# Hybrid decoder layer on one core: three plain column blocks in place of two ahead of the seven-product loop, and a later split of the first down chunk

## The chip, the cores and the metric

One core of one Trainium2 chip. The metric is the device time of one execution in microseconds (us), as the median of several runs; a profile of one execution stands beside it.

## The reference

One layer on 512 tokens of width 1024, float32: a mixer with attention and retention heads, then cross-attention to 256 memory rows, then a gated feed-forward part, each with a norm ahead, a norm behind and a residual. The change lies in the feed-forward part and in the last rows of the cross-attention ahead of it:

```python
FFN_HIDDEN = 2816

def swiglu(h, w_gate_up, w_down):
    g, u = jnp.split(h @ w_gate_up, 2, axis=-1)
    return (jax.nn.silu(g) * u) @ w_down

y = memory_cross_attn(rms_norm(x, pre_mem_g[l]), mem, mem_norm_g[l],
                      w_q_mem[l], w_kv_mem[l], w_o_mem[l])
x = x + rms_norm(y, post_mem_g[l])
y = swiglu(rms_norm(x, pre_ffn_g[l]), w_gate_up[l], w_down[l])
x = x + rms_norm(y, post_ffn_g[l])
```

## The kernel before

Each float32 operand is split into a high part and the rest (`split`, lines 88 to 94: ScalarE casts, VectorE subtracts), and each product is three matmuls (`mm3`, lines 82 to 86): high by high, high by rest, rest by high.

The tokens are four row blocks of 128. `mem_block` (line 855) does the out projection of the cross-attention for one row block, its residual and the next norm, and gives `h`. `to_b` (line 861) transposes `h` on TensorE and splits it into `B11` and `B21` (row blocks 0 and 1, the two halves of the width) or `B12` and `B22` (row blocks 2 and 3). For row blocks 2 and 3 it also forms `t1` to `t4`, differences of these. Their splits into `T1` to `T4` come later (`late_splits`). Row block 2 does its subtractions on GpSimd, row block 3 on VectorE.

The hidden width of 2816 is 22 column blocks of 128, numbered `f`. Each has 128 gate columns and 128 up columns, which lie in HBM as four parts a11, a12, a22, a21 of 512. Gate and up for all tokens are a product of two 2 by 2 block matrices, and there are two ways to get it:

- `plain` (line 993): eight block products, 24 matmuls of 256 columns for each of gate and up and for each half of the tokens, 96 in all. Its first half (`n` 0) needs row blocks 0 and 1 alone, the second (`n` 1) needs `B12` and `B22`. It takes a pair `was[f]` over all 2048 columns, made by `blocks_a(f, 2048, 512)`.
- `step` (line 948): seven block products with sums of blocks, 84 matmuls of 256 columns. It takes `was[f]` over 1536 columns and `wbs[f]`, the split of `sums[f]`.

`blocks_fetch` (line 110) loads a raw block from SP's queue into one of two buffers. `blocks_a` (line 127) casts it on ScalarE (L131), negates the cast (L134), and lets an accumulating DMA from GpSimd's queue add the raw block from HBM to it (L135), so that the rest is left. `blocks_sum` (line 115) forms s1 and s2 on VectorE, s3 and s4 on GpSimd. `blocks_b` splits one half of the sums.

Blocks 0 and 1 are plain (`PRE = 2`, line 991). The order written at lines 1000 to 1031 is: fetch and `blocks_a` of both, fetch of block 2, first halves of both with `to_b` of row block 2 between them, `to_b` of row block 3, `blocks_a` and sums of block 2, second halves of both, each followed by the silu product (L1023, L1024) and its store, then block 3. Here a scheduler orders the instructions when it compiles, by program order and by when it takes them to be ready. Blocks 2 to 21 run in `step` under a fixed order, the order of the text.

Within a step, products 1 and 2 go to the two halves of bank `p`. ScalarE copies the first half to `s1` (`ffn_c1`, line 927), and VectorE adds the second half (`ffn_c11`, line 931, the addition `c L933`). Products 4 and 6 go to `q` and `r`, then `s L979` reads `r`; 5 goes to `q`; 7 overwrites the first half of `p`; 3 goes to the second half of `r`. Between the copy and the addition the step splits half of the next block's sums. In block 21 there is no next block, and `load()` (line 142), which splits the first chunk of w_down, stands there instead:

```python
    if nxt:
        blocks_b(f + 1, 1)
    else:
        load()
    ffn_c11(f)
    q, r = bank("q2"), bank("r")
```

SBUF holds twenty units of 8 KB a partition (`unit`, line 57): a pair is two of them, a chunk of w_o is a pair, x is two units of two row blocks. x is stored to HBM (L1034) before the loop, which frees its units. PSUM has eight banks (`bank`, line 54).

After the loop the down projection (`down`, line 1061) runs 528 matmuls of 512 columns, and the last residual ends the kernel.

Of the kernel before, what the change touches and what calls it, by code (L numbers as in the profile page):

```python
# [38 lines left out]
def hybrid_layer(ctx, tc, t, out):  # L39
# [10 lines left out]
    def uname(p):  # L50
        cnt[0] += 1
        return f"{p}{cnt[0]}"

    def bank(name):
        return psp.tile([P, 512], F32, tag="ps", name=uname(name))

    def unit(name, dt=F32):
        return up.tile([P, 2048], dt, tag="u", name=uname(name))

    def pair(name):  # L60
        return unit(name + "h", F32R), unit(name + "l", F32R)

    def work(name):
        return wk.tile([P, 512], F32, tag="w2k", name=uname(name))
# [14 lines left out]
    def part(pr, c0, n):  # L79
        return pr[0][:, c0:c0 + n], pr[1][:, c0:c0 + n]  # L80
# [7 lines left out]
    def split(src, hi, lo, scale=None):  # L88
        if scale is None:
            nc.scalar.copy(hi, src)  # L90
            nc.vector.tensor_sub(lo, src, hi.bitcast(F32))  # L91
        else:
            nc.scalar.mul(hi, src, scale)
            nc.vector.scalar_tensor_tensor(lo, src, scale, hi.bitcast(F32), op0=ALU.mult, op1=ALU.subtract)
# [6 lines left out]
    def fetch(key):  # L101
        fetched[key] = raw = rawp.tile([P, 2048], F32, tag="raw", name=uname("raw"))
        nc.sync.dma_start(raw, t[key[0]][key[1]])
# [6 lines left out]
    def blocks_fetch(f):  # L110
        chunks.remove(("w_gu", f))
        raws[f] = rawp.tile([P, 2048], F32, tag="raw", name=uname("raw"))
        nc.sync.dma_start(raws[f], t["w_gu"][f])

    def blocks_sum(f, names):
        if f not in sums:
            sums[f] = unit("sums")
        a11, a12, a22, a21 = (raws[f][:, i * 512:(i + 1) * 512] for i in range(4))
        s2, s4, s1, s3 = (sums[f][:, i * 512:(i + 1) * 512] for i in range(4))
        for name in names:  # L120
            e = nc.gpsimd if name in ('s3', 's4') else nc.vector
            if name == "s1":
                e.tensor_add(s1, a21, a22)
            else:
                e.tensor_sub(*{"s2": (s2, s1, a11), "s3": (s3, a11, a21), "s4": (s4, a12, s2)}[name])  # L125

    def blocks_a(f, n=1536, m=768):
        w = was[f] = pair("wa")
        for c0 in range(0, n, m):
            c = slice(c0, c0 + m)  # L130
            nc.scalar.copy(w[0][:, c], raws[f][:, c])  # L131
        for c0 in range(0, n, m):
            c = slice(c0, c0 + m)
            nc.scalar.mul(w[1][:, c], w[0][:, c].bitcast(F32), -1.0)  # L134
        nc.gpsimd.dma_start(w[1][:, :n], t["w_gu"][f][:, :n], accum_op=ALU.add)  # L135

    def blocks_b(f, i):
        if f not in wbs:
            wbs[f] = pair("wb")
        split(sums[f][:, i * 1024:(i + 1) * 1024], *part(wbs[f], i * 1024, 1024))  # L140

    def load(pieces=1, swap=False):
        key = chunks.pop(0)
        src = t[key[0]][key[1]]
        raw = fetched.pop(key, None)
        w = pair("w")
        if raw is None:
            raw = rawp.tile([P, 2048], F32, tag="raw", name=uname("raw"))
            n = 2048 // pieces
            for i in range(pieces):  # L150
                c = slice(i * n, (i + 1) * n)
                nc.sync.dma_start(raw[:, c], src[:, c])
        n = 2048 // max(2, pieces)
        for i in range(max(2, pieces)):
            c = slice(i * n, (i + 1) * n)
            if swap and i == 0:
                nc.vector.tensor_copy(w[0][:, c], raw[:, c])
                nc.vector.tensor_sub(w[1][:, c], raw[:, c], w[0][:, c].bitcast(F32))
            else:
                split(raw[:, c], w[0][:, c], w[1][:, c])  # L160
        loaded[key] = w
# [750 lines left out]
    def product(i, w, ps):  # L912
        u, c0, name = prods[i]
        for k in range(4):
            x_ = bx[name][:, k * H:(k + 1) * H], bx[name][:, 1024 + k * H:1024 + (k + 1) * H]
            mm3(ps, part(w[u], c0 + k * P, P), x_, k == 0, k == 3)
# [3 lines left out]
    def ffn_p12(f):  # L920

        w, p = (was[f], wbs[f]), bank("p")
        product(1, w, p[:, :H])
        product(2, w, p[:, H:])
        ffn[f] = w, p, work("s1"), work("c"), work("u")

    def ffn_c1(f):
        w, p, s1, c, u = ffn[f]
        nc.scalar.copy(s1[:, :H], p[:, :H])

    def ffn_c11(f):
        w, p, s1, c, u = ffn[f]
        nc.vector.tensor_add(c[:, :H], s1[:, :H], p[:, H:])  # L933

    def ffn_done(f):
        w, p, s1, c, u, r = ffn[f]
        nc.vector.tensor_add(c[:, H:], c[:, H:], r[:, H:])  # L937
        nc.scalar.activation(c, c, AF.Silu)  # L938

    def keep(f, v):  # L940
        nc.sync.dma_start(ad[:, f * S:(f + 1) * S], v)

    def ffn_mult(f):
        c, u = ffn.pop(f)[3:5]
        nc.vector.tensor_mul(c, c, u)
        keep(f, c)

    def step(f):
        nxt = f + 1 < FT
        two = f + 2 < FT  # L950
        ffn_p12(f)
        w, p, s1, c, u = ffn[f]
        if f + 3 < FT:
            blocks_fetch(f + 3)
        else:
            fetch(("w_dn", f + 3 - FT))
        if f > PRE:
            ffn_done(f - 1)
        if two:
            blocks_sum(f + 2, ("s3", "s1", "s2"))  # L960
        ffn_c1(f)
        if f > PRE:
            ffn_mult(f - 1)
        if nxt:
            blocks_b(f + 1, 1)
        else:
            load()
        ffn_c11(f)
        q, r = bank("q2"), bank("r")
        ffn[f] += (r,)  # L970
        product(4, w, q[:, :H])
        product(6, w, r[:, :H])
        if two:
            blocks_sum(f + 2, ("s4",))
        if nxt:
            blocks_b(f + 1, 0)
        if two:
            blocks_a(f + 2)
        nc.vector.tensor_add(s1[:, H:], s1[:, :H], r[:, :H])  # L979
        product(5, w, q[:, H:])  # L980
        nc.vector.tensor_add(c[:, H:], s1[:, H:], q[:, H:])
        product(7, w, p[:, :H])
        nc.vector.tensor_add(s1[:, :H], s1[:, H:], p[:, :H])
        nc.vector.tensor_add(u.rearrange("p (i s) -> p i s", i=2), q.rearrange("p (i s) -> p i s", i=2),
                             s1[:, None, :H].to_broadcast([P, 2, H]))
        product(3, w, r[:, H:])
        for d in (raws, was, sums, wbs):
            d.pop(f, None)


    PRE = 2

    def plain(f, j, n, ps):
        for i, (c0, name) in enumerate(((0, "B1%d"), (512, "B2%d")) if j == 0 else ((1536, "B1%d"), (1024, "B2%d"))):
            v = bx[name % (n + 1)]
            for k in range(4):
                mm3(ps[:, n * H:(n + 1) * H], part(was[f], c0 + k * P, P),
                    (v[:, k * H:(k + 1) * H], v[:, 1024 + k * H:1024 + (k + 1) * H]), i == k == 0, i == 1 and k == 3)

    pg = {f: (bank("g"), bank("u")) for f in range(PRE)}  # L1000
    for f in range(PRE):
        blocks_fetch(f)
        blocks_a(f, 2048, 512)
    blocks_fetch(2)
    for f in range(PRE):
        for j in range(2):
            plain(f, j, 0, pg[f][j])
        if f == 0:
            late_splits = [to_b(hb, 2, nc.gpsimd)]
    late_splits.append(to_b(hc, 3))  # L1010
    blocks_a(2)
    blocks_sum(2, ("s3", "s1", "s2", "s4"))
    blocks_fetch(3)
    for f in range(PRE):
        for j in range(2):
            plain(f, j, 1, pg[f][j])
        if f == 0:
            for e in late_splits:
                e()
            late_splits.clear()  # L1020
        del was[f], raws[f]
        sg = work("sg")
        nc.scalar.activation(sg, pg[f][0], AF.Silu)  # L1023
        nc.vector.tensor_mul(sg, sg, pg[f][1])  # L1024
        keep(f, sg)
        blocks_b(2, 1 - f)
    pg.clear()
    del bx["B12"]
    blocks_a(3)
    blocks_sum(3, ("s3", "s1", "s2", "s4"))  # L1030
    blocks_fetch(4)
    xd = tc.dram_tile([S, D], F32, name="xd")
    for b in range(TB):
        nc.sync.dma_start(xd[b * P:(b + 1) * P, :], x[b])  # L1034
# [13 lines left out]
    with tc.manual_schedule():  # L1048
        for f in range(PRE, FT):
            step(f)  # L1050
            if f == FT - 2:
                split_a(0)
        ffn_done(FT - 1)
        ffn_mult(FT - 1)
# [130 lines left out]
```

## Time and profile before

| what | us |
|---|---|
| median of 3 runs | 802.81 |
| all runs | 955.97, 802.81, 799.59 |
| profiled execution, own time | 801.05 |
| its span, first to last instruction | 799.3 |
| TensorE busy in the span | 780.2 |
| VectorE busy | 502.5 |
| ScalarE busy | 386.4 |
| GpSimd busy | 201.1 |
| DMA, mean of the span | 151 GB/s |

Matmuls overlap one another, and each is shown longer than its distance to the next; the distance is read from starts. The feed-forward part begins at 439.69 with the first plain block; the loop runs from 465.25 to 672.23, the down projection from 672.23 to 792.11.

### The profile page before, as it was taken

Reading aid. Unit: us, or ns where it says so; the run is one execution under the profiler, and the core shown is the slowest. Engines: PE = TensorE matmul, PEld = TensorE weight load, DVE = VectorE, ACT = ScalarE, POOL = GpSimd, SP = SyncE. Lnnn points to the kernel's source line nnn. Section 1 sums busy time; section 2 is a strip of 40 time slices with the busy share of each in tenths; the row PEclk is TensorE's granted clock in tenths of the full one; section 3 lists DMA queues with packets and bytes.
Section 4 is the critical chain, followed back from the end, with each engine's and each line's share of the span. In section 5 each row is a group of like instructions: output and inputs, shape, how many; then the busy total and the mean of one; then the engine's idle time right before and its main releaser. Section 6 shows DMA issues by size and latency. Waiting matters only on the chain.

```text
span 799.3 us, 12220 instructions
## 1 busy us (share of the span) xinstructions
PE 780.2 (98%) x4828; PEld 695.8 (87%) x4828; DVE 502.5 (63%) x1002; ACT 386.4 (48%) x667; POOL 201.1 (25%) x177
## 2 busy tenths in 40 slices
PE   9999999899999999999999989999999999999996
PEld 7788888777887888999988989999999998888885
DVE  6497368574666657757567797667777767541143
ACT  6522424485563824445437575555555545542011
POOL 0163033420111100400000654333333326551000
PEclk9999999989999999999999999999999999999999
DMA  8634313223135430525008288777777793864011
GB/s 324 268 132 155 109 53 106 66 79 119 54 106 204 170 154 0 182 83 192 19 28 214 80 243 220 208 210 206 208 208 205 208 267 117 310 250 171 1 52 53
DMA packets 24489, 120.60 MB, mean 151 GB/s; under 512 B 2928, under 2 KB 2928, under 8 KB 14960
## 3 DMA queue, kind: packets, MB, share of 16 engines
q1 hardware_dynamic: 19904, 99.89, 34.3%
q0 software_dynamic: 3808, 18.88, 12.6%
q10 hardware_dynamic: 720, 1.06, 0.4%
q8 instruction: 38, 0.62, 0.3%
q14 instruction: 19, 0.16, 0.1%
HBM read 108.80 MB, written 9.96 MB: 149 GB/s over the span
## 4 chain that ended last, share of the span: by engine, by line
PE 52%; DVE 4%; issue 0%; ACT 0%; DVEq 0%; ACTq 0%
PE dn L84 5%; PE dn L85 5%; PE dn L86 5%; PE p L84 3%; PE p L86 3%; PE p L85 3%; PE q L85 3%; PE q L86 3%; PE q L84 3%; PE r L84 2%; PE r L86 2%; PE r L85 2%; PE o L84 2%; PE o L85 2%; PE o L86 2%; DVE wbl L91 1%
## 5 line engine op out<-in xcount | busy, mean ns | idle before, releaser
L91 DVE TENSOR_TENSOR wl<-raw,wh 128x1024 fp32r<-128x1024 f32 (+1 forms) x91 | 120.0, 1354 | 69.1 <-ACT wh L90 39.0
L90 ACT CAST wh<-raw 128x1024 fp32r<-128x1024 f32 (+1 forms) x91 | 90.0, 1038 | 61.4 <-DMA raw<-in_w_in 29.3
L91 DVE TENSOR_TENSOR wbl<-sums,wbh 128x1024 fp32r<-128x1024 f32 x40 | 51.2, 1280 | 30.3 <-ACT wbh L90 30.3
L84 PE MATMUL dn<-wh,ah 128*128 128x512 f32 x176 | 68.5, 389 | 0.0
L85 PE MATMUL dn<-wl,ah 128*128 128x512 f32 x176 | 68.5, 389 | 0.0
L86 PE MATMUL dn<-wh,al 128*128 128x512 f32 x176 | 68.5, 389 | 0.0
L135 POOL DMA_DIRECT2D wal<-in_w_gu x22 | 19.5, 887 | 176.1 <-ACT wal L134 117.5
L1045 POOL TENSOR_TENSOR al<-af,ah 128x512 fp32r<-128x512 f32 x22 | 36.1, 1673 | 43.9 <-ACT ah L1044 43.9
L84 PE MATMUL p<-bB,wah 128*128 128x256 f32 x160 | 45.3, 283 | 0.0
L85 PE MATMUL p<-bB,wah 128*128 128x256 f32 x160 | 45.3, 283 | 0.0
L86 PE MATMUL p<-bB,wal 128*128 128x256 f32 x160 | 45.3, 283 | 0.0
L90 ACT CAST wbh<-sums 128x1024 fp32r<-128x1024 f32 x40 | 40.2, 1051 | 3.4 <-POOL sums L125 1.8
L125 POOL TENSOR_TENSOR sums<-raw,sums 128x512 f32<-128x512 f32 x20 | 34.1, 1705 | 25.4 <-DVE sums L125 25.4
L86 PEld LDWEIGHTS dn<-wh,al 128*128 128x128 f32 x176 | 33.0, 188 | 6.9
L84 PEld LDWEIGHTS dn<-wh,ah 128*128 128x128 f32 x176 | 33.0, 188 | 6.8
L85 PEld LDWEIGHTS dn<-wl,ah 128*128 128x128 f32 x176 | 33.0, 188 | 6.8
L134 ACT ACTIVATE wal<-wah 128x768 fp32r<-128x768 f32 (+1 forms) x48 | 36.6, 809 | 0.0
L85 PE MATMUL q<-hhl,wh 128*128 128x256 f32 x128 | 36.2, 284 | 0.2 <-DVE hhl L91 0.2
L938 ACT ACTIVATE c<-c 128x512 f32<-128x512 f32 x20 | 12.7, 632 | 49.1 <-DVE c L937 49.1
L84 PE MATMUL q<-hhh,wh 128*128 128x256 f32 x128 | 35.8, 284 | 0.3 <-ACT hhh L90 0.3
L86 PE MATMUL q<-hhh,wl 128*128 128x256 f32 x128 | 36.1, 283 | 0.0
L131 ACT CAST wah<-raw 128x768 fp32r<-128x768 f32 (+1 forms) x48 | 35.9, 803 | 0.0
(346 smaller groups left out, 2521.5 us busy)
## 6 DMA issues: line engine op xcount, KB each, us to landing
raw<-in_w_gu SPq DMA_DIRECT2D x22, 1024.0 KB, 4.9
wal<-in_w_gu POOLq DMA_DIRECT2D x20, 768.0 KB, 7.3
raw<-in_w_in SPq DMA_DIRECT2D x12, 1024.0 KB, 5.0
raw<-in_w_dn SPq DMA_DIRECT2D x11, 1024.0 KB, 5.0
raw<-in_w_kv SPq DMA_DIRECT2D x8, 1024.0 KB, 4.7
ad<-c SPq DMA_DIRECT2D x20, 256.0 KB, 4.0
af<-ad SPq DMA_DIRECT2D x5, 1024.0 KB, 7.3
x<-in_x SPq DMA_DIRECT2D x4, 1024.0 KB, 9.5
```

Of the source, the lines that this page charges most:

```text
L84: nc.tensor.matmul(o, lhsT=sh, rhs=mh, start=start, stop=False)
L85: nc.tensor.matmul(o, lhsT=sh, rhs=ml, start=False, stop=False)
L86: nc.tensor.matmul(o, lhsT=sl, rhs=mh, start=False, stop=stop)
L90: nc.scalar.copy(hi, src)
L91: nc.vector.tensor_sub(lo, src, hi.bitcast(F32))
L125: e.tensor_sub(*{"s2": (s2, s1, a11), "s3": (s3, a11, a21), "s4": (s4, a12, s2)}[name])
L131: nc.scalar.copy(w[0][:, c], raws[f][:, c])
L134: nc.scalar.mul(w[1][:, c], w[0][:, c].bitcast(F32), -1.0)
L135: nc.gpsimd.dma_start(w[1][:, :n], t["w_gu"][f][:, :n], accum_op=ALU.add)
L938: nc.scalar.activation(c, c, AF.Silu)
L1045: nc.gpsimd.tensor_sub(lo[:, c], v[:, c], hi[:, c].bitcast(F32))
```

## The change

The number of plain blocks, `PRE`, becomes 3, and what followed from it by number is written with `PRE`: the loop begins with block 3, the three plain blocks have their first halves in a row (with `to_b` of row block 2 after that of block 0) and then their second halves, and block 3 and 4 are prepared where 2 and 3 were. The two halves of the first loop block's sums are now split after the second and the third plain block. In the last step `load()` now follows `ffn_c11`.

```diff
@@ def step(f)
         if nxt:
             blocks_b(f + 1, 1)
-        else:
+        ffn_c11(f)
+        if not nxt:
             load()
-        ffn_c11(f)
         q, r = bank("q2"), bank("r")
...
-    PRE = 2
+    PRE = 3
...
     for f in range(PRE):
         blocks_fetch(f)
         blocks_a(f, 2048, 512)
-    blocks_fetch(2)
+    blocks_fetch(PRE)
     for f in range(PRE):
         for j in range(2):
             plain(f, j, 0, pg[f][j])
         if f == 0:
             late_splits = [to_b(hb, 2, nc.gpsimd)]
     late_splits.append(to_b(hc, 3))
-    blocks_a(2)
-    blocks_sum(2, ("s3", "s1", "s2", "s4"))
-    blocks_fetch(3)
+    blocks_a(PRE)
+    blocks_sum(PRE, ("s3", "s1", "s2", "s4"))
+    blocks_fetch(PRE + 1)
     for f in range(PRE):
         for j in range(2):
             plain(f, j, 1, pg[f][j])
...
         keep(f, sg)
-        blocks_b(2, 1 - f)
+        if f:
+            blocks_b(PRE, 2 - f)
     pg.clear()
     del bx["B12"]
-    blocks_a(3)
-    blocks_sum(3, ("s3", "s1", "s2", "s4"))
-    blocks_fetch(4)
+    blocks_a(PRE + 1)
+    blocks_sum(PRE + 1, ("s3", "s1", "s2", "s4"))
+    blocks_fetch(PRE + 2)
```

## Rows read from the trace of the kernel before

**Rows 1.** The page's first part: busy us (share), instructions of each engine.

```profile
PE 780.2 (98%) x4828; PEld 695.8 (87%) x4828; DVE 502.5 (63%) x1002; ACT 386.4 (48%) x667; POOL 201.1 (25%) x177
```

**Rows 2.** Stretches: length, then busy us of each engine (the first line names them).

```profile
core 0: us, PE busy (x) PEld busy (x) DVE busy (x) ACT busy (x) POOL busy (x), PEclk, DMA share, GB/s
453.33:465.25 11.92, 11.84 (x96) 11.67 (x97) 11.79 (x14) 11.62 (x19) 8.70 (x7) 1.00 0.49 109
465.25:478.82 13.57, 10.81 (x86) 10.23 (x85) 13.42 (x17) 9.01 (x12) 7.24 (x6) 1.00 0.81 243
650.18:660.26 10.08, 10.08 (x86) 10.08 (x85) 5.67 (x9) 2.97 (x4) 0.00 (x0) 1.00 1.03 325
660.26:672.23 11.97, 10.30 (x86) 10.13 (x85) 7.85 (x9) 6.55 (x11) 10.99 (x7) 1.00 0.25 68
672.23:792.11 119.88, 119.87 (x530) 98.95 (x528) 46.28 (x66) 34.56 (x52) 25.13 (x16) 1.00 0.38 145
```

**Rows 3.** Chain of waits in order of time: start, us, engine, tile, line.

```profile
474.68 0.33 DVE c L933
...
664.70 4.12 DVE wl L91 x2
...
668.82 0.34 DVE c L933
```

**Rows 4.** Timeline of TensorE: start, us, instruction [idle before it <- releaser].

```profile
428.71 0.48 PE L84 MATMUL o<-wh,oTxh 128*128 128x512 f32 x1
...
452.06 1.04 PE L868 MATMUL tp<-ident,h 128*128 128x128 f32 x8
...
472.71 0.28 PE L86 MATMUL q<-bT,wbl 128*128 128x256 f32 x1
...
475.15 0.35 PE L84 MATMUL p<-bT,wbh 128*128 128x256 f32 x1 [2.16 <-DVE c L933]
...
667.35 0.28 PE L86 MATMUL q<-bT,wbl 128*128 128x256 f32 x1
...
669.29 0.35 PE L84 MATMUL p<-bT,wbh 128*128 128x256 f32 x1 [1.67 <-DVE c L933]
```

**Rows 5.** Timeline of VectorE.

```profile
453.31 1.29 DVE L886 TENSOR_TENSOR bB<-tp,bB 128x512 fp32r<-128x512 f32 x2 [2.94 <-ACT bB L885]
...
467.73 0.67 DVE L1024 TENSOR_TENSOR sg<-sg,u 128x512 f32<-128x512 f32 x1
...
654.69 1.23 DVE L91 TENSOR_TENSOR wbl<-sums,wbh 128x1024 fp32r<-128x1024 f32 x1 [2.50 <-ACT wbh L90]
...
663.23 1.11 DVE L945 TENSOR_TENSOR c<-c,u 128x512 f32<-128x512 f32 x1 [2.34 <-ACT c L938]
...
669.07 0.41 DVE L979 TENSOR_TENSOR s<-s,r 128x256 f32<-128x256 f32 x1
```

**Rows 6.** Timeline of ScalarE.

```profile
425.78 2.19 ACT L131 CAST wah<-raw 128x512 fp32r<-128x512 f32 x4
...
429.90 1.19 ACT L134 ACTIVATE wal<-wah 128x512 fp32r<-128x512 f32 x2
...
439.94 0.60 ACT L687 ACTIVATE junk<-o 128x512 bf16<-128x512 f32 x1 [3.75 <-PE o L86]
...
663.35 0.37 ACT L929 COPY s<-p 128x256 f32<-128x256 f32 x1
```

**Rows 7.** DMA issues from 400 to 480: count, KB each, median us to landing.

```profile
wal<-in_w_gu POOLq DMA_DIRECT2D x2, 1024.0 KB, 11.3
```

**Rows 8.** Timeline of SP's queue.

```profile
422.22 0.33 SPq L113 DMA_DIRECT2D raw<-in_w_gu  x1
422.59 0.43 SPq L1034 DMA_DIRECT2D xd<-x  x1
```

**Rows 9.** Timeline of GpSimd (POOL).

```profile
446.74 1.29 POOL L890 TENSOR_TENSOR t<-b,braw 128x512 f32<-128x512 f32 x1 [12.98 <-ACT b L880]
...
661.24 11.22 POOL L1045 TENSOR_TENSOR al<-af,ah 128x512 fp32r<-128x512 f32 x7 [11.43 <-ACT ah L1044]
```

## The prediction

> **What bounds the kernel now.** I read the page's first part, the stretches, the chain of waits in order of time, and then each engine's own timeline around the two places that the change touches. TensorE is busy for 98% of the span [rows 1], so only work taken from TensorE, or a gap on it, can change the time. The stretches show where the gaps are. A seven-product block of the loop, 84 matmuls of 256 columns, takes 10.08 us when nothing holds it, from 650.18 to 660.26 [rows 2], which is 120 ns for one matmul. The granted clock is 1.00 in every stretch I use, the higher of its two levels, so the clock plays no part.
>
> Two blocks are longer. The first one (block 2) runs from 465.25 to 478.82, 13.57 us, 3.49 us too long. The last one (block 21) runs from 660.26 to 672.23, 11.97 us, 1.89 us too long [rows 2]. After it the down projection runs 119.88 us with TensorE busy for 119.87, so time won ahead of it should arrive at the end undiminished [rows 2].
>
> The chain of waits says why. In both blocks it leaves TensorE and goes through VectorE to `c L933`, the addition in ffn_c11, which reads the bank `p` that product 7 is about to overwrite [rows 3]. In block 2 the last matmul of product 5 starts at 472.71, and product 7 starts only at 475.15, after 2.16 us of idle put down to that addition [rows 4]. Its successor `s L979` is then late too and holds product 3; the rest of the 3.49 us is that and a small wait for a split in product 6. VectorE hardly rests there: it waits 2.94 us for the transposed columns of row block 3, gets them at 453.31 [rows 5], and is then busy for 11.79 of 11.92 us and for 13.42 of 13.57 us [rows 2]. In block 21 the addition stands behind two splits of the first w_down chunk, 4.12 us from 664.70, and product 7 waits 1.67 us for it [rows 3, 4].
>
> **The change, part by part.**
>
> *Third plain block, cost.* A plain block is 2 outputs x 2 halves x 8 row tiles x 3 = 96 matmuls, a seven-product block 84. Twelve more at 120 ns: +1.44 us of TensorE. (The Trainium skill, TensorE: Matmul & The Clock Gate, Back-to-back issue gap, gives N / 2.4 + 2.5 ns, 109 ns for 256 columns, by which I estimate the twelve at 1.31 us. The trace has 120 ns, so this formula is a little short here, and the row decides.)
>
> *Third plain block, gain.* Block 2's products leave the loop; the loop starts at block 3. The first halves of the plain blocks don't need row blocks 2 and 3, the second halves do. One more first half, 48 matmuls or 5.76 us, goes ahead of the transposes of row block 3, and one more second half behind them. So VectorE's long run starts 5.76 us later, but product 7 of the first loop block comes 11.52 us later. To its run I add one more silu product, 0.67 us [rows 5]; the sums, the eight splits and the halves of the seven-product weights are as many as before, for block 3 in place of block 2. The addition, which ended at 475.01 [rows 3], then ends at 475.01 + 5.76 + 0.67 = 481.44, and TensorE, which wanted it at 472.83, wants it at 472.83 + 11.52 = 484.35. It is early by 2.9 us without any credit for VectorE's idle time before 453.31, in which sums of block 3 could now be done. So the 3.49 us go altogether: bounds 0 and 3.49, I take 3.49.
>
> The third block also costs ScalarE four casts and four negations of 512 columns, 2.19 us and about 2.4 us (1.19 for two) [rows 6]. ScalarE has 3.75 us of idle ahead of 439.94 [rows 6]; the rest would push the row statistics of row block 3 by under 1 us, and its columns are now transposed 5.76 us later than the 452.06 of before [rows 4]. One more silu, about 0.6 us, sits in a stretch where ScalarE feeds VectorE, which has the 2.9 us. DMA gains 256 KB: block 2's accumulate becomes 1024 KB in place of 768 KB. Its raw fetch, issued at 422.22, is the same [rows 8]. On SP the fetch of block 4 now waits for the casts of block 2 alone, so it goes out earlier, and the extra store of a silu product stands behind nothing that TensorE needs. In POOL's queue the accumulate stands ahead of the subtractions for row block 2, which start at 446.74 [rows 9].
>
> Its cover is the question. The accumulate takes 11.3 us when it runs beside other transfers [rows 7], and block 2's first half starts where row block 3's transposes start today, 452.06 [rows 4], with the accumulated copy needed at its third matmul, 452.3. It needs two of the twenty 8 KB units. By the code, one comes free with x's first half after its store, issued at 422.59 [rows 8], and two with w_o's first chunk after its last matmul: the last out projection starts at 428.71 [rows 4], and 30 matmuls of 227 ns (119.88 us for the 528 of the down projection) [rows 2] later it is 435.5. ScalarE is in its own work until 436.19, where its 3.75 us of idle begin; negations of 2.4 us from there end at 438.6, and 11.3 us later is 449.9: 2.4 us in hand. Bounds: 0 and, if both units come only at the end of the out projection, a stall of 4.2 us (below). I take 0, since the earlier units are the nearer reading.
>
> *Addition ahead of the load in block 21.* The addition needs `s1`, copied by ScalarE at 663.35 for 0.37 us [rows 6], and a free VectorE, which finishes the product before it at 664.34 [rows 5]. It then ends at about 664.75, and the first split, which starts at 664.70 today, loses next to nothing. The splits end where they do now, 668.8. Behind them stands `s L979`, which product 3 waits for: today it starts at 669.07 [rows 5], then it takes the addition's place at 668.8 and lets TensorE go at 669.29, as the addition did. Product 7 now starts at 667.47 and ends its issue at 668.91. So the stall moves to product 3 and shrinks from 1.89 to 669.29 - 668.91 + 0.07 = 0.45 us (0.07 is what the restart cost product 7: 1.89 less the 1.82 between 667.47 and 669.29). Gain 1.44 us; bounds 0, if the order on VectorE stays, and 1.89. No DMA moves: the chunk was fetched earlier, and the next fetch waits for the same splits.
>
> Why the two splits take 2.06 us each, where 1024 columns take 1.23 alone [rows 5], is seen on POOL: seven subtractions run beside them [rows 9]. The Trainium skill, SBUF — State Buffer, Who interferes with whom, has it that a VectorE operation with two SBUF inputs and a GpSimd one that reads SBUF shut each other out. By that rule the sums and splits that now fall into POOL's work for row block 2 would be slowed too, which speaks against the change; the second rival has it, priced from rows.
>
> *Sum.* 801.05 (the profiled execution: span 799.3, 1.75 around it) + 1.44 - 3.49 - 1.44 = 797.56, say 797.6. The median of the runs shown, 802.81, is 0.2% above the profiled execution, and the lowest, 799.59, as much below; I stay with the sum.
>
> **The rivals.**
>
> 1. *The accumulate is late (the other side).* ScalarE's four casts and four negations come only after the out projection's last matmul: from about 440.6, when the row statistics at 439.94 are through [rows 6], so the accumulate goes out at 445.2 and lands at 456.5, 4.2 us after block 2's third matmul wants it. For it: all twenty units look taken until 435, and the two such accumulates before took 11.3 us. Against it: ScalarE's idle stretch before 439.94. Time 797.6 + 4.2 = 801.8, slower than before by 0.7; it ends slower from a landing after 455.8.
>
> 2. *VectorE is still late.* Beside POOL a split takes 2.06 us in place of 1.23, 0.83 more [rows 3, 5]. If four more operations of the run fall beside POOL's work, that is 3.3 us, over the 2.9 us in hand, and product 7 of block 3 waits again. With the whole stall back, which takes some 6.4 us (2.9 + 3.49): 801.05 + 1.44 - 1.44 = 801.1. For it: the run is all but unbroken for 21 us [rows 2]. Against: nothing is added to it but 0.67 us, and POOL was at work for 8.70 and 7.24 us beside it already [rows 2].
>
> 3. *More than I count.* If row block 3's transposes are put ahead of the third first half, their cast and subtraction are hidden and VectorE starts at once: between 453.33 and 465.25 the second halves take 11.92 us for 96 matmuls, 11.52 at 120 ns [rows 2], and ahead of them 1.27 us go by from the start of eight transposes at 452.06 [rows 4], of which a wait is part. Gain 1.0 us at most, an estimate from these two: 796.6.
>
> 4. *The load's new place does nothing.* If the splits still go first, or product 3 waits as long as product 7 did, 1.44 us stay: 799.0.
>
> **How the numbers follow.** My forecast 0.62, rival 1 0.16, rival 2 0.08, rival 3 0.07, rival 4 0.05. What is left, 0.02, is a rearrangement of the whole stretch before the loop that costs over 16 us; nothing in the rows points to it. Runs of the kernel before spread by about 1.6 us either side of the profiled one, which I add outside the cases: 796.6 less 1.5 gives 795.1, and rival 1's 801.8 with part of the spread 802.4. The range is 795.1 to 802.4. A measurement of this kernel tells about 2%, 16 us, from no change, and every case but the last lies within that: faster 0.01, same 0.97, slower 0.02.
>
> **What would show it.** Right: no idle put down to `c L933` in the first and in the last loop block; the first loop block 10.1 us long; a wait of about 0.4 us for `s L979` ahead of product 3 in block 21; first half of block 2 without a gap at its third matmul. Wrong: a gap there put down to the accumulate or to its negation (rival 1), `c L933` in the first loop block (rival 2), or TensorE idle inside the down projection, which would mean that w_down chunks come too late for an earlier start.

## The result and the profile after

The changed kernel takes 795.63 us (median of 4 runs, 795.42 to 796.51), the kernel before, run beside it, 802.01 (4 runs, 799.59 to 955.97; the ratio leaves the 955.97 out, and the median of the other three is 801.22). The ratio is 0.9932, interval 0.9906 to 0.9959: a little faster, and not by more than the 2% that the prediction named as what can be told. 797.6 was predicted, with a range of 795.1 to 802.4. The sum was made against profiled executions: 801.05 before, 795.68 after, 5.4 us less where 3.5 was expected.

The page's first part, busy us of each engine, answers to [rows 1]: twelve more matmuls, as counted, and 2.1 us less of TensorE's busy time.

```profile
PE 778.1 (98%) x4840; PEld 694.5 (87%) x4840; DVE 495.2 (62%) x992; ACT 384.6 (48%) x668; POOL 197.5 (25%) x175
```

**First, what is not the change's.** Both programs do the same work up to the first plain block, yet that block starts at 439.69 before and at 436.80 after. The difference is made far from the change: 0.5 us in the first microseconds, 2.8 between 161 and 168, and 0.4 given back near 286. This is the stretch from 160 to 170 of the kernel before; the granted clock, 0.66, stands behind the engines' busy times:

```profile
160.00:170.00 10.00, 8.45 (x25) 6.74 (x26) 8.11 (x25) 6.27 (x14) 4.45 (x6) 0.66 0.27 53
```

The same stretch of the changed kernel:

```profile
160.00:170.00 10.00, 8.91 (x39) 7.43 (x40) 8.12 (x26) 6.23 (x15) 4.17 (x5) 1.00 0.26 53
```

In both executions TensorE has just been idle for 2.9 us, waiting for a tile of the attention (the kernel before, then the changed one):

```profile
161.55 0.80 PE L84 MATMUL av<-wh,hTh 128*128 128x512 f32 x1 [2.92 <-DVE t L458]
161.09 0.50 PE L84 MATMUL av<-wh,hTh 128*128 128x512 f32 x1 [2.89 <-DVE t L458]
```

After it the granted clock is 1.00 in the changed kernel, the higher of the two levels (2.4 and 1.2 GHz). The 0.66 of the kernel before is a mean of both: its matmuls of 512 columns start 0.43 us apart up to 167.3 and 0.23 apart behind it. So times are compared from here on from the first plain block's first matmul. From there to the first matmul of the down projection it is 232.54 us before (439.69 to 672.23) and 230.06 after (436.80 to 666.86). The change's own share is 2.48 us, not 5.4, and 3.49 was predicted. The likeliest number was near, and part of that nearness is luck.

**Stretches.** They answer to [rows 2]: the first halves up to row block 3's columns, the second halves, the first loop block, a block without a wait, the last block, the down projection (length, then busy us of TensorE, its weight loads, VectorE, ScalarE, GpSimd).

```profile
436.80:456.19 19.39, 19.16 (x161) 18.92 (x159) 7.91 (x24) 4.56 (x10) 9.78 (x7) 1.00 0.67 189
456.19:473.60 17.41, 17.41 (x144) 17.39 (x145) 17.02 (x22) 15.91 (x24) 8.28 (x6) 1.00 0.50 136
473.64:483.72 10.08, 10.08 (x87) 10.08 (x86) 6.38 (x11) 5.21 (x7) 3.80 (x3) 1.00 0.93 253
...
644.99:655.07 10.08, 10.08 (x86) 10.08 (x85) 5.67 (x9) 2.90 (x4) 0.00 (x0) 1.00 1.02 312
655.07:666.86 11.79, 10.34 (x86) 10.14 (x85) 7.80 (x9) 6.43 (x11) 9.52 (x6) 1.00 0.18 49
666.86:786.70 119.84, 119.84 (x530) 98.92 (x528) 47.30 (x66) 34.55 (x52) 26.90 (x17) 1.00 0.39 148
```

The first loop block has gone from 13.57 us to 10.08, as long as a block that nothing holds. The last one has gone from 11.97 only to 11.79. The down projection, 119.84 for 119.88, hands on what was won ahead of it.

TensorE's waits between 436 and 669 that are listed (waited for, total us, times, longest) show what is left:

```profile
PE r L84 <- DVE s L979: 1.4, 1, 1.4
PE g L84 <- ACT bB L885: 0.2, 1, 0.2
```

The stall of [rows 3, 4] in the first loop block is gone. In the last block it has moved from product 7 to product 3, as predicted, with 1.45 us in place of 0.45. The timelines of VectorE, of ScalarE and of TensorE there:

```profile
659.33 1.13 DVE L945 TENSOR_TENSOR c<-c,u 128x512 f32<-128x512 f32 x1 [3.63 <-ACT c L938]
660.38 0.41 DVE L933 TENSOR_TENSOR c<-s,p 128x256 f32<-128x256 f32 x1
660.72 4.22 DVE L91 TENSOR_TENSOR wl<-raw,wh 128x1024 fp32r<-128x1024 f32 x2
664.86 0.41 DVE L979 TENSOR_TENSOR s<-s,r 128x256 f32<-128x256 f32 x1
...
656.58 2.18 ACT L1045 CAST ah<-af 128x512 fp32r<-128x512 f32 x4 [6.24 <-DMA af<-ad]
658.67 0.63 ACT L938 ACTIVATE c<-c 128x512 f32<-128x512 f32 x1
659.20 0.35 ACT L929 COPY s<-p 128x256 f32<-128x256 f32 x1
659.46 2.00 ACT L90 CAST wh<-raw 128x1024 fp32r<-128x1024 f32 x2
...
665.32 0.39 PE L84 MATMUL r<-bB,wbh 128*128 128x256 f32 x1 [1.45 <-DVE s L979]
```

Read ScalarE from the top. Its first work in the last block are four casts of `af`, the first chunk of the silu products, which comes back from HBM (L1042, issued in block 20). ScalarE works in the order of the text here: the silu of block 20 (`c L938`) had its input at 655.69, while ScalarE was idle, and still ran only behind the casts, at 658.67. Behind it stand the copy `s1` that the addition wants, and the casts that the two splits want. The reload landed late, the casts began 1.51 us into the block, and the splits 5.65 us into it. In the kernel before these were 0.22 and 4.44 (664.70 [rows 3], with the block's start at 660.26). ScalarE there:

```profile
660.48 2.18 ACT L1044 CAST ah<-af 128x512 fp32r<-128x512 f32 x4 [4.87 <-DMA af<-ad]
```

The chain of waits of the changed kernel, from 647.46 on, names the same transfer:

```profile
647.46 9.04 DMA af<-ad
```

I had taken the splits' start as fixed. In this execution a transfer sets it.

### The profile page after: what moved, and what is told of

It is laid out like the page before. It is cut to its first block, busy times and chain, and to the rows that moved or that the text cites. A ratio compares the mean times of both kernels' runs of the same rounds, so it can differ in the third digit from the quotient of the medians.

```text
span 793.9 us, 12232 instructions
## 1 busy us (share of the span) xinstructions
PE 778.1 (98%) x4840; PEld 694.5 (87%) x4840; DVE 495.2 (62%) x992; ACT 384.6 (48%) x668; POOL 197.5 (25%) x175
## 3 DMA queue, kind: packets, MB, share of 16 engines
q0 software_dynamic: 3808, 19.14, 13.3%
## 4 chain that ended last, share of the span: by engine, by line
PE 53%; DVE 2%; DMA 1%; ACT 0%; issue 0%; DVEq 0%; SPq 0%; ACTq 0%
PE dn L85 5%; PE dn L86 5%; PE dn L84 5%; PE p L86 3%; PE p L85 3%; PE p L84 3%; PE q L85 3%; PE q L86 3%; PE q L84 3%; PE r L84 2%; PE r L86 2%; PE r L85 2%; PE o L86 2%; PE o L84 2%; PE o L85 2%; DMA af<-ad 1%
## 5 line engine op out<-in xcount | busy, mean ns | idle before, releaser
L91 DVE TENSOR_TENSOR wbl<-sums,wbh 128x1024 fp32r<-128x1024 f32 x38 | 46.5, 1226 | 30.9 <-ACT wbh L90 30.9
L84 PE MATMUL p<-bB,wah 128*128 128x256 f32 x152 | 43.0, 283 | 0.0
L85 PE MATMUL p<-bB,wah 128*128 128x256 f32 x152 | 43.0, 283 | 0.0
L86 PE MATMUL p<-bB,wal 128*128 128x256 f32 x152 | 43.0, 283 | 0.0
L90 ACT CAST wbh<-sums 128x1024 fp32r<-128x1024 f32 x38 | 38.0, 1051 | 0.0
L125 POOL TENSOR_TENSOR sums<-raw,sums 128x512 f32<-128x512 f32 x19 | 31.4, 1657 | 22.7 <-DVE sums L125 22.6
L938 ACT ACTIVATE c<-c 128x512 f32<-128x512 f32 x19 | 12.0, 632 | 46.1 <-DVE c L937 46.1
```

The source lines that it names most:

```text
L84: nc.tensor.matmul(o, lhsT=sh, rhs=mh, start=start, stop=False)
L85: nc.tensor.matmul(o, lhsT=sh, rhs=ml, start=False, stop=False)
L86: nc.tensor.matmul(o, lhsT=sl, rhs=mh, start=False, stop=stop)
```

## The experiments

Four questions are asked: what each half of the change does alone, whether the reload ate the second half's gain, how close the accumulate of rival 1 came, and how much VectorE had in hand. The medians are of whole executions; "aligned" is from the first plain block's first matmul to the first `dn` matmul of the profiled one, which leaves the clock of 160 to 170 out. The first four ran on one chip and the last four on another, each group beside the kernel before.

| kernel | median us (runs) | before, beside it | ratio, interval | aligned us | last block us |
|---|---|---|---|---|---|
| before | | | | 232.54 | 11.97 |
| after | 795.63 (4) | 802.01 | 0.9932, 0.9906 to 0.9959 | 230.06 | 11.79 |
| e1_third_block_only | 797.0 (8) | 800.41 | 0.9953, 0.9932 to 0.9973 | 229.85 | 11.56 |
| e2_addition_first_only | 798.52 (12) | 800.41 | 0.9972, 0.9957 to 0.9988 | 232.40 | 11.83 |
| e3_both_again | 796.65 (10) | 800.41 | 0.9946, 0.9929 to 0.9964 | 229.24 | 10.95 |
| e4_early_reload | 795.39 (6) | 800.41 | 0.9932, 0.9908 to 0.9956 | 228.36 | 10.08 |
| e5_casts_twice | 795.86 (1) | 799.68 | single run | 230.35 | 10.20 |
| e6_early_reload_old_order | 795.59 (6) | 799.68 | 0.9939, 0.9919 to 0.9959 | 228.50 | 10.20 |
| e7_splits_twice | 797.58 (1) | 799.68 | single run | 231.90 | 10.21 |
| e8_before_again | 799.4 (1) | 799.68 | single run | 232.36 | 11.78 |

**The third plain block alone** (`load()` stays ahead of the addition):

```diff
-        ffn_c11(f)
-        if not nxt:
+        else:
             load()
+        ffn_c11(f)
```

> Three plain blocks, the load in its old place ahead of the addition. Theory (two separate terms, each on TensorE's path): the first loop block is 10.1 us long, the last one is again held by the addition behind the two splits. Its length is then the start of the first split after the block's start, plus 4.2 us of splits, 0.45 us, and products 7 and 3 (2.88 us): 11.9 us if that start is 4.4 us after the block's start as in the kernel before, 13.1 us if it is 5.65 us as in the changed kernel. Time 1.4 us over the changed kernel in the same runs, 2 us under the kernel before. Rival (the load's new place does nothing): the same time as the changed kernel within 0.3 us.

Measured: aligned 229.85, 2.69 less than before. The first loop block shows no wait. 0.41 of the 2.69 are a shorter last block (11.56 for 11.97), so the third plain block gave about 2.28; the prediction had 3.49 - 1.44 = 2.05. The time was a miss: the median is 3.4 us under that of before, where 2 was expected, and only 0.35 over the changed kernel's in the same runs (796.65), where 1.4 was expected. The runs of the two kernels spread over 4.7 and 3.8 us, and the medians can't tell 0.35 from 0 or from 1.4. What the load's new place is worth is read from the last blocks below, and not from these times. In the last block the wait of before is still there, on product 7:

```profile
659.10 3.71 DVE L91 TENSOR_TENSOR wl<-raw,wh 128x1024 fp32r<-128x1024 f32 x2 [0.79 <-ACT wh L90]
662.73 0.41 DVE L933 TENSOR_TENSOR c<-s,p 128x256 f32<-128x256 f32 x1
...
663.28 0.36 PE L84 MATMUL p<-bT,wbh 128*128 128x256 f32 x1 [1.26 <-DVE c L933]
```

**The addition first, alone** (two plain blocks):

```diff
-    PRE = 3
+    PRE = 2
...
-        if f:
-            blocks_b(PRE, 2 - f)
+        blocks_b(2, 1 - f)
```

> Two plain blocks as before, only the addition moved ahead of the load. Theory: the first loop block keeps its 13.6 us; the last has the wait at product 3 instead of product 7 and is one product, 1.44 us, shorter at the same start of the splits: 10.5 us with splits from 4.4 us after its start, 11.7 us with 5.65 us. Time 1.4 us under the kernel before. Rival A (the new place does nothing): same time as before. Rival B (the reload of the first gate blocks sets the end of the last block, and its landing differs from execution to execution): the last block lies between 10.5 and 11.9 us and the split's start follows the landing of that reload.

Measured: the first loop block waits as before (2.2 us for `c L933`), and in this profiled execution the last block is 11.83 us, hardly shorter than the 11.97 before. Product 3 waits 1.50 us for `s L979`. The casts of the reload say why (ScalarE); the block starts at 660.20:

```profile
661.77 2.18 ACT L1044 CAST ah<-af 128x512 fp32r<-128x512 f32 x4 [6.21 <-DMA af<-ad]
```

They begin 1.57 us into the block, as in the trace of the changed kernel (1.51), and the splits 5.69 us into it. The median is 1.9 below that of before all the same (ratio 0.9972). The profiled execution, 800.85, is the slowest of the twelve; that the others got the reload sooner is likely and not shown.

**Both again**, the changed kernel itself, beside the two:

> The changed kernel once more, for its scatter. Theory (the late reload in the last block and the clock near 160 us in the kernel before were chance of single executions): the reload lands 7.8 to 9.4 us after its issue, the last block is 10.5 to 11.8 us long with it, and the first loop block is 10.1 us again. Rival (the later landing belongs to the changed kernel): 9.2 us from issue to landing again and a last block of 11.8 us. Time 5 us under the kernel before if the granted clock stays high from 160 to 170 us, 2 to 3.5 us under it if both kernels have the same clock there.

Measured: aligned 229.24, 3.30 less than before, and the last block is 10.95 us where the first profile of the same kernel had 11.79. The program has not changed by an instruction. The reload landed 7.2 us after its issue (9.2 in the first profile), the casts began 0.55 us ahead of the block's start at 657.92, and the splits 4.43 behind it. ScalarE, VectorE and TensorE:

```profile
657.37 2.18 ACT L1045 CAST ah<-af 128x512 fp32r<-128x512 f32 x4 [4.18 <-DMA af<-ad]
...
661.41 0.42 DVE L933 TENSOR_TENSOR c<-s,p 128x256 f32<-128x256 f32 x1 [0.19 <-ACT s L929]
662.35 4.61 DVE L91 TENSOR_TENSOR wl<-raw,wh 128x1024 fp32r<-128x1024 f32 x2 [0.53 <-ACT wh L90]
666.88 0.41 DVE L979 TENSOR_TENSOR s<-s,r 128x256 f32<-128x256 f32 x1
...
667.34 0.39 PE L84 MATMUL r<-bB,wbh 128*128 128x256 f32 x1 [0.62 <-DVE s L979]
```

The granted clock from 160 to 170 is 0.66 in this execution: the dip of the kernel before, in the changed kernel.

**The reload one block early.** If its landing is the cause, issuing the same transfer before block 20's step in place of behind it, with its casts left where they are, must empty the last block of waits:

```diff
         for f in range(PRE, FT):
+            if f == FT - 2:
+                v0 = load_a(0)
             step(f)
             if f == FT - 2:
-                split_a(0)
+                split_a(0, v0)
```

> The changed kernel, with the reload of the first four gate blocks from HBM issued one loop block earlier, the casts of it where they were. Theory (ScalarE's casts of that reload stand ahead of the silu, the copy and the casts of the first w_down chunk in the last block, so its landing sets that block): the casts run before block 21 starts, the first split starts about 4.4 us after the block's start or earlier, bound by the copy (3.1 us) and by the splits; the wait at product 3 falls from 1.5 us to 0.5 us or less; time 1.0 to 1.5 us under the changed kernel. Rival (the splits are late for another reason, such as GpSimd's subtractions beside them): the wait at product 3 stays over 1 us and the time is the same. A loss would show as a wait for the last accumulate at the start of block 21, since the reload then runs beside it.

Measured: it does. The last block is 10.08 us, aligned 228.36 (4.18 less than before), and the median 795.39, 5.0 below that of before beside it. The profiled execution, 793.28, is the fastest of its six. ScalarE's casts are now done ahead of the block, which starts at 654.38, and the two splits are short (ScalarE, VectorE):

```profile
649.54 2.18 ACT L1051 CAST ah<-af 128x512 fp32r<-128x512 f32 x4
...
657.46 0.37 ACT L929 COPY s<-p 128x256 f32<-128x256 f32 x1 [1.79 <-PE p L86]
...
658.81 2.36 DVE L91 TENSOR_TENSOR wl<-raw,wh 128x1024 fp32r<-128x1024 f32 x2 [0.53 <-ACT wh L90]
```

The block as a stretch, in which TensorE rests for nothing:

```profile
654.38:664.46 10.08, 10.08 (x86) 10.08 (x85) 6.26 (x9) 4.46 (x7) 6.04 (x5) 1.00 0.23 54
```

GpSimd's four subtractions of the chunk ran from 650.31 to 656.34, ahead of the splits and not beside them.

The start of the splits did not move: 4.43 us into the block, as in the second profile of the changed kernel. It has a floor that no transfer sets, the copy of `s1`, which waits for TensorE's second product and starts 3.08 us into the block here. Six of the eight profiles without the early reload have the splits at this floor (4.43 to 4.44), the kernel before among them; in the other two (5.65 and 5.69) the reload landed too late. So the reload costs in two ways. GpSimd's work on it beside the splits makes them longer, which against the second profile is the whole of the 0.87 us won here (10.95 to 10.08, splits of 4.61 and 2.36). A landing 1.5 us behind the block's start also makes them late, by 1.22 us in the first profile.

**The early reload with the old order.** Does the addition's place still matter then?

```diff
-        ffn_c11(f)
-        if not nxt:
+        else:
             load()
+        ffn_c11(f)
```

> The early reload with the load in its old place, ahead of the addition, and three plain blocks. Theory (the addition's place matters only because the reload lets ScalarE's casts, and so the splits, run late): with the reload early, the splits take 2.4 us from 4.4 us after the block's start, the addition ends about 7.2 us after it, where product 7 wants it (7.2 us), and the last block is 10.1 to 10.4 us long; time within 0.4 us of the early reload with the new order. Rival (two separate gains): the last block is 11.5 us long, and the time 1.4 us more.

Measured: hardly. The last block is 10.20 us, aligned 228.50, the median 795.59 (on the other chip; 0.9939 of before there, 0.9932 for the early reload with the new order); no wait is listed in it. The addition comes in time for product 7, which starts at 664.18 (VectorE):

```profile
661.35 2.36 DVE L91 TENSOR_TENSOR wl<-raw,wh 128x1024 fp32r<-128x1024 f32 x2 [1.92 <-ACT wh L90]
663.62 0.41 DVE L933 TENSOR_TENSOR c<-s,p 128x256 f32<-128x256 f32 x1
```

With the reload out of the way the order of the two is worth 0.12 us, and with the reload where it is about 1.4 to 1.6 (predicted 1.44): at the same start of the splits (4.43) and nearly the same length of the two (3.7 to 3.9) the old order gives 11.56 and 11.78 (third block alone, before again), the new one 10.20 and 10.21 (the two kernels that follow).

**The accumulate of block 2, 1.9 us later.** For rival 1 the four casts ahead of its accumulate are made twice, which changes no value:

```diff
-        for c0 in range(0, n, m):
+        for c0 in [*range(0, n, m)] * (2 if f == 2 else 1):
```

> The changed kernel, with ScalarE's four casts of block 2, the third plain block, made twice (2.2 us of extra work that changes no value). It delays the block's negations and its accumulate, the step of which the prediction said 2.4 us are in hand. In the changed kernel's trace the accumulate was issued at 435.80 and landed 13.3 us later, at 449.1, against a third matmul of block 2's first half at 449.4. Theory (that step has next to nothing in hand): TensorE waits 1.5 to 2 us at that matmul. Rival (the landing is late only because of transfers beside it, and a later issue lands sooner after it): a wait under 0.7 us.

Measured: the accumulate goes out at 437.69 in place of 435.80, lands 13.2 us later, and TensorE waits for it at the third matmul, just where rival 1 had put its wait. GpSimd's issue and TensorE:

```profile
437.69 0.86 POOL L135 DMA_DIRECT2D wal<-in_w_gu  x1 [6.96 <-ACT wal L134]
...
451.08 0.36 PE L86 MATMUL g<-bB,wal 128*128 128x256 f32 x1 [1.64 <-DMA wal<-in_w_gu]
```

The landing, 450.9, comes 0.2 ahead of the matmul that it lets go. In the changed kernel it is 449.1 for a matmul at 449.40, so of the 0.3 us there only about 0.1 is a margin. From the first plain block to the loop it is 38.71 us for 36.83, 1.88 more, and 230.35 less 1.88 is 228.47: the prediction's 229.05 less 0.25 for the waited-for columns (below) and less 0.33 for a last block of 10.20 in place of 10.53.

**VectorE burdened by some 5 us.** The eight subtractions of row block 2's and 3's `T` are made twice, which changes no value either:

```diff
+                split(v, hi, lo)
+                nc.vector.tensor_sub(lo, v, hi.bitcast(F32))
```

> The changed kernel, with VectorE's eight subtractions for T1 to T4 made twice (8 x 0.75, about 6 us more in its run ahead of the loop, no value changed). In the changed kernel VectorE had 2.6 us of idle ahead of the addition of the first loop block, and the addition was over 1.2 us before product 7 wanted it: 3.8 us in hand. Theory (the wait is gone because VectorE's run now fits): with 6 us more, product 7 of the first loop block waits about 2.2 us for the addition again, and the first loop block is 12 to 13 us long. Rival (the wait went for another reason, such as fewer transfers or GpSimd work beside it): under 0.5 us of wait.

Measured: the wait for the addition is back, but smaller than expected. The sixteen subtractions take 10.74 us, the eight of the changed kernel 5.93, so 4.8 more, and the work between them and the addition takes 0.3 more: 5.1 in all and not 6. VectorE runs all but unbroken up to 485.96. TensorE (lines are six further down in this kernel):

```profile
482.09 0.36 PE L84 MATMUL p<-bT,wbh 128*128 128x256 f32 x1 [1.02 <-DVE c L939]
484.23 0.39 PE L84 MATMUL r<-bB,wbh 128*128 128x256 f32 x1 [0.48 <-DVE s L985]
487.14 0.38 PE L86 MATMUL p<-bB,wal 128*128 128x256 f32 x1 [0.99 <-DMA wal<-in_w_gu]
```

Product 7 starts at 482.09; in the changed kernel it is 480.83, and this loop starts 0.08 later (473.71), so it is 1.2 us late. 5.1 of work less 1.2 leaves 3.9 us that VectorE had in hand. The third wait, for the next block's accumulate, I had not expected.

**Before again**, for the scatter of one kernel:

> The kernel before once more, for the scatter of what the change does not touch. Theory (chance of single executions): the first loop block is 13.6 us again; the last one is 11.5 to 13.2 us, following the landing of the reload (7.2 to 9.4 us after issue); the granted clock from 160 to 170 us is 0.66 or 1.00, and the start of the first plain block moves by 2.9 us with it. Rival: both the same as in the first trace, which would tie them to the kernel.

Measured: aligned 232.36 (232.54 in the first profile), both old stalls, and a granted clock of 0.83 from 160 to 170 where it was 0.66 (0.66 or 1.00 was expected). The first plain block starts at 438.19, between the 439.69 of before and the 436.80 of after.

## Why the prediction was right, and where it was not

**What bounds it: right.** The aligned time changed by twelve matmuls and by gaps on TensorE, and by nothing else: 1.19 us more for the added block, 3.49 less in the first loop block and 0.18 less in the last, 2.48 less together. That "the clock plays no part" held for the stretches that the prediction used; in the comparison of the two profiled executions the clock far ahead of them has some 3 us.

**Cost of the third plain block: 1.44 predicted, about 1.2 measured.** From the first plain block to the loop it is 25.56 us before and 36.83 after, +11.27, where 11.52 at 120 ns had been counted; the loop has one block of 10.08 less. The missing 0.25 is the wait for row block 3's columns, partly covered now. VectorE still has to subtract them, and six high by high matmuls, which don't need the difference, are put ahead:

```profile
456.19 0.39 PE L84 MATMUL g<-bB,wah 128*128 128x256 f32 x1 [0.24 <-ACT bB L885]
456.42 0.28 PE L84 MATMUL u<-bB,wah 128*128 128x256 f32 x1
...
457.01 0.36 PE L85 MATMUL g<-bB,wah 128*128 128x256 f32 x1
```

That is a small piece of rival 3 by another way. The rest of that rival did not come: the transposes follow the third first half (454.92), as the forecast had it.

**Stall of the first loop block: right.** 3.49 us gone, block 10.08 us long, no wait. The prediction gave VectorE 2.9 us in hand. The trace has the addition ended at 479.63, 1.20 ahead of product 7 at 480.83, and 2.61 us of idle on VectorE just before, 3.81 together; the burdened kernel puts it at 3.9. VectorE and TensorE of the changed kernel:

```profile
478.07 1.23 DVE L91 TENSOR_TENSOR wbl<-sums,wbh 128x1024 fp32r<-128x1024 f32 x1 [2.61 <-ACT wbh L90]
479.21 0.42 DVE L933 TENSOR_TENSOR c<-s,p 128x256 f32<-128x256 f32 x1
...
480.83 0.28 PE L84 MATMUL p<-bT,wbh 128*128 128x256 f32 x1
```

Rival 2 (VectorE still late) falls with it.

**The accumulate: outcome right, margin wrong.** It went out at 435.80, 0.1 us from the 438.6 of the prediction when the 2.9 us of the earlier start are taken off, so the reading of units and of ScalarE's idle stretch held. But it landed 13.3 us later and not 11.3 [rows 7], at 449.1, for a matmul at 449.40: 0.1 to 0.3 us in hand, not 2.4. The term that failed is the transfer's length, read off two transfers with other neighbours: in all seven profiles with three plain blocks the accumulate of block 2 took 12.5 to 13.3 us. One neighbour is new by the change itself, the fetch of block 4, which goes out at 431.79 where it was 460.83; the prediction saw that it would go out earlier and gave it no price. That it is the cause is not shown. The delayed kernel shows it as a wait. With the 0.16 that it had, rival 1 was priced too cheap for so small a margin; the profiles of the changed kernel itself, both of them, show no such wait.

**The addition ahead of the load: mechanism right, size wrong in the profiled execution.** The stall moved to product 3 as said. It was to shrink from 1.89 to 0.45 us; it is 1.45 at the wait, and the block 1.71 over 10.08. The step that failed is "the splits end where they do now": their start, 4.44 us into the block, stood for a constant, and is the later of two, the copy of `s1` behind TensorE's second product (which gives 4.43) and the landing of the reload plus what ScalarE has in its order behind it (5.65 here). In the kernel before the two came out together, so its trace alone could not tell them apart. I had read ScalarE for when `s1` is copied and VectorE for when it is free, and not asked what ScalarE's own first instruction of the block waits for, though its timeline in the trace of before names that DMA too (4.87 us of idle ahead of the casts at 660.48). Where the reload is on time, the term is right within 0.4: 10.95 in the second profile of the same kernel, 10.20 and 10.21 in the kernels with the casts and with the subtractions made twice, where 10.53 was predicted; the splits' length, 3.85 to 4.61, makes the difference. Rival 4 (the new place does nothing) falls by the last blocks at one start of the splits, 11.56 to 11.97 with the old order against these, and not by the medians of whole executions. What made the reload land 7.2 us after issue in one execution and 9.2 in another isn't settled.

**Why the splits are slow: right.** The prediction put their length down to GpSimd's subtractions beside them. Two take 2.36 us (early reload, 658.81) where GpSimd's next subtraction starts only at 660.38, 0.8 us before their end, as 1.23 for one [rows 5] would have it, and 3.71 to 4.61 with subtractions beside them from the start. The Trainium skill, SBUF — State Buffer, Who interferes with whom, says that a VectorE operation with two SBUF inputs and a GpSimd one that reads SBUF shut each other out; these rows agree with it.

**The sum.** 232.54 - 3.49 = 229.05 was predicted for the aligned stretch. Measured: 230.06 and 229.24 for the two profiles of the changed kernel, 1.0 and 0.2 above. Both follow from the last block and the 0.25 of the columns: it was 1.26 longer than predicted in the first (the late reload) and 0.42 in the second (two splits of 4.61 us). The medians of the runs made together, 800.41 and 796.65, differ by 3.8. The rest of the 5.4 us between the first two profiled executions is the clock of 160 to 170 and the start, which no step of mine concerned. On the aligned stretch the forecast was a little too low, so that the measured time came out 2 us below 797.6, and not above it, is luck.

**A version that beats both.** The changed kernel with the early reload: 795.39 beside 796.65 and 800.41 on the same chip. Against the kernel before its interval is clear; against the changed one the intervals overlap, and what speaks for it is the last block without a wait, 0.9 to 1.7 us shorter.

## What to carry to other kernels

Before an order on one engine is priced, follow the engine that feeds it back to its own first instruction: the engine may hold the work that matters behind a cast that waits for a transfer, and then that transfer's issue is the thing to move. A start that looks constant in one trace can be the later of two that happen to agree. Take a transfer's length from neighbours that are the same, and give a margin of 2 us on a landing the spread that such landings have in the trace. Compare two profiles from the last common point on, and repeat the profile before believing a difference of a few us: a stretch far away can shift everything behind it.

## What the runs showed of the hardware

After the same 2.9 us of idle TensorE, which ends between 160.9 and 161.6, the granted clock of the stretch from 160 to 170 differs between executions and not between kernels: 0.66 in the profiles of before, of the addition alone and of both again, 0.83 in before again and the early reload with the old order, 1.00 in the other five. The first plain block starts at 439.6 to 439.7, 438.2 to 438.6 and 436.1 to 436.9 in these three groups, so some 3 us hang on it. What decides it no run here shows.

A reload of 1 MB from HBM landed 7.2 us after issue in one execution and 9.2 in another of the same program. In the eight executions with the reload in its old place it took 7.2 to 9.3 us (each the median of two such transfers). The accumulating transfer of 1 MB for block 2 took 12.5 to 13.3 us in the seven profiles with three plain blocks, where two in the kernel before had a median of 11.3 [rows 7].

A subtraction of 1024 columns on VectorE takes 1.2 us by itself, and 1.9 to 2.3 us where GpSimd subtracts beside it.
